# A two-layer gMLP and forgetting-attention trunk on one core: x loaded ahead of small broadcasts, the residual reloaded in mixer 2, one finished tile per unit of the last product, key projection ahead of the first softmax

## The chip, the cores and the metric

The kernel runs on one core of a Trainium2 chip. Its metric is the device time of one execution in microseconds (us). Before the change that is 2215.34 us, the median of three runs (2212.86 to 2218.98). The core's engines each work through a queue of their own: TensorE (PE) multiplies matrices, VectorE (DVE), ScalarE (ACT) and GpSimd (POOL) work on tiles in SBUF and PSUM, and SyncE (SP) issues most of the transfers (DMAs) between DRAM and SBUF.

## The reference

The input x is 1024 tokens of width 1024, all fp32. Two layers work on it, one after the other. What they compute, cut to its core:

```python
# layer A: gMLP mixer and memory attention, then a gated FFN with a causal convolution
z = rmsnorm(x, a_norm1) @ a_w_in                      # 768 u, 768 v, 256 memory queries
u, vv, q_mem = gelu(z[:768]), gelu(z[768:1536]), z[1536:]
tok = u * (tril(w_s) @ rmsnorm(vv, v_norm) + b_s)     # blocks of 128 tokens, 4 groups
x = x + concat(tok, memory_attention(q_mem, mem)) @ a_w_out
x = x + conv_ffn(rmsnorm(x, a_norm2), ...)            # 1024 -> 2 x 2816 -> 1024
# shared keys, values and forget gates, from the x of here
kvf = rmsnorm(x, kv_norm) @ w_kv                      # 768 k, 768 v, 12 gate logits
log_f_cum = cumsum(log_sigmoid(f_logit + b_f))
# layer B: causal attention with a decay bias, 12 heads of 64, and memory attention
z = rmsnorm(x, b_norm1) @ b_w_q                       # 768 q, 256 memory queries
logits = q @ k.T / 8 + log_f_cum[q] - log_f_cum[k]    # causal
x = x + concat(softmax(logits) @ v, memory_attention(...)) @ b_w_out
x = x + conv_ffn(rmsnorm(x, b_norm2), ...)
out = rmsnorm(x, final_norm)
```

## The kernel before

Every fp32 operand of a large product is split in two parts, a rounded high part and the rest (`split_to`, `split_new`, `wconv`, `opnd`: ACT casts the high part, DVE or POOL subtracts it for the low one), and each product is three matmuls: high by high, high by low, low by high. TensorE has 10,657 matmuls and transposes in all. SBUF tiles of 128 rows by 1024 fp32 (512 KB) come from one pool of 33 buffers, drawn with `xt_()` and named X in the profile; a new tile waits until the buffer that it gets is no longer read. Tiles of the tag `nb` have three buffers.

The Python code emits the instructions of all engines, and a scheduler arranges each engine's queue when the kernel is built, except for those marked with `tc.keep_in_program_order`: these keep the order in which the code emits them. The matmuls and transposes of the mixers are marked so while `strict[0]` is set, and loads made with `ld` while `dpin[0]` is set:

```python
        ins = nc.sync.dma_start(dst, src)
        if dpin[0]:
            tc.keep_in_program_order(ins)
```

**The start.** SP loads weights and x tiles (line 184, in `ld`). `x_in(i)` squares two token tiles on ACT, transposes them on PE and splits them into `xh`, `xl`; behind each pair, `vv_g` makes the first v projections of these tokens (lines 1077 to 1080). `dpin[0] = False` stands at line 1055, ahead of that loop. The broadcasts of a_b_s into `bsb` (line 1122, eight loads) and of b_f into `bf` (line 1226) are emitted later; the mixer and the gate logits read them.

**The FFN.** `ffn` is used by both layers. Its output product, `out_phase`, is cut in halves of its three dimensions and made of seven block products in place of eight: p1, p5, p6, p3, p7, p2 and p4, each over NU = 6 units of up to two 128-deep blocks. `prep` loads and splits the operands of a unit AHEAD = 2 units before it is multiplied; `both(x, y, pool)` splits x and y, one of them on POOL where `pool` is true (x in layer A, y in layer B, where `tm` is true), lines 799 and 800 are the cast and the subtraction. p2 ends the first four tiles of the result (`acc[0]` to `acc[3]`): `take` adds the bank of PSUM, and `on_done(j, acc[j])` hands the tile on. p4, the last product, ends the other four; its last TAILU = 2 units run tile by tile:

```python
            for j in range(4):
                on_done(j, acc[j])
            for u in range(NU - TAILU):
                run(a, "p4", u, False)
                before_last(u + 1)
```

In layer A `on_done` is `done_a`: the tile is split (`nh`, `nl`) and its square is added to a running sum (ACT squares, POOL adds, line 342). In layer B it is `finish`, the last norm and the store.

**The entry into attention.** Behind the first projections of layer B come the gate logits `fz`, log-sigmoid on ACT and DVE, VPRE = 8 steps of `mem_v` (three 256-wide matmuls each) on PE, the transposes of the gates, a scan on DVE, and a store and broadcasts of the sums by way of DRAM (`cdram`). Then LOOK first steps of scores (`s_tasks`) are emitted, and the next key and query projection, `proj_kq`, is drawn ahead until its own count of time reaches PRE = 5000 ns, in steps of 432 ns.

**The attention loop.** 48 steps (a head and a pair of query blocks each) merge scores, softmax and values; projections that are still to be made (`fills`) are laid between them, at a rate that spreads what is left of each over the steps up to its due step.

**The second mixer.** `tail` loads each head pair's attention result `o` from DRAM and splits it, and rebuilds the residual x from its halves, one tile per `merge_next`, with a POOL addition (line 1600):

```python
        eng.tensor_tensor(t, f32(xl[n]), f32(xh[n]), ALU.add)
```

The merged result is multiplied with `b_w_out` (`mix_part`, `mix_out`), and the second FFN follows. `xdram` is a DRAM buffer for x, to which the mixers store it and from which `load_xT` reads it for the FFN's sum.

Of the kernel before, what the change touches and what calls it, by code (L numbers as in the profile page):

```python
# [13 lines left out]
ALU = mybir.AluOpType  # L14
AX = mybir.AxisListType

P = 128
# [25 lines left out]
TRATE = 1.0  # L43
KQD = 5
EVY = 0
PRE = 5000.0
MQD = (41, 45)
MEMT = 45
CONVK = 12
VPRE = 8  # L50
NORD = (0, 4, 1, 5, 2, 6, 3, 7)
POOLED = (0, 3, 4, 5, 6)
HK = NFF // 2
# [6 lines left out]
def kernel(  # L60
# [33 lines left out]
    nc = tc.nc  # L94
# [22 lines left out]
    def xt_(dt=F32, shape=(P, S)):  # L117
        return xp.tile(list(shape), dt, tag="X", name=nm("X"))
# [12 lines left out]
    def f32(ap):  # L131
        return ap.bitcast(F32)
# [48 lines left out]
    dpin = [False]  # L181

    def ld(dst, src):
# [3 lines that stand above are left out]
# [330 lines left out]
    def drain(g):  # L517
        for _ in g:
            pass
# [154 lines left out]
    def ffn(ops, ssum, first, w_out, cvs, on_done, tp, tm, before_last=lambda stage: None):  # L674
# [128 lines left out]
        def both(x, y, pool=False):  # L803
            return opnd(x, pool and not tm), opnd(y, pool and tm)

        def tt(out, x, y, op=ALU.subtract):
            nc.vector.tensor_tensor(out, x, y, op)  # L807
            return out
# [3 lines left out]
        def prep(name, u):  # L812
# [30 lines left out]
            if name == "p2":  # L843
                return both(la(0, 1, u), lb(1, 0, u), True)
            a22, b21 = la(1, 1, u), lb(1, 0, u)
            return both(a22, tt(b21, b21, kept[u][1]), True)

        steps = [("p1", u) for u in range(NU)]
        for u in range(NU + 1):
# [55 lines left out]
        def out_phase(cg):  # L905
# [4 lines left out]
            def run(bank, p, u, start):  # L910
                i = steps.index((p, u))
                ahead(i + 1 + AHEAD)
                op = ready.pop((p, u))
                for j in range(4):
                    mms(bank, op, u, j, start)
# [35 lines left out]
                if u == 2:  # L951
                    before_last(0)
            take(c, 0, 0)
            for j in range(4):
                on_done(j, acc[j])
            for u in range(NU - TAILU):
                run(a, "p4", u, False)
                before_last(u + 1)
            ahead(len(steps))
            for j in range(4):  # L960
# [91 lines left out]
    ws_raw = tp.tile([P, 4, P], F32, tag="T2", name="ws_raw", bufs=3)  # L1052
    ld(ws_raw, a_w_s[0].rearrange("g t s -> t g s"))

    dpin[0] = False
    vg = {}
    sv = cp.tile([P, KT, 3], F32, name="sv")

# [18 lines left out]
    for i in range(4):  # L1077
        if i < 3:
            x_in(i + 1)
        drain(vv_g(0, (2 * i, 2 * i + 1)))  # L1080
    rm = mem_norm(tp, mtok, "P", pbufs[0])
    rb = cp.tile([P, S], F32, name="rb_a", tag="rb", bufs=1)

# [35 lines left out]
               [(2, 0, P)], [(2, 0, 64), (3, 64, P)], [(3, 0, P)]]  # L1119
    for f in range(6):  # L1120
        for g, lo_, hi_ in fgroups[f]:
            ld(bsb[lo_:hi_, f, :], a_b_s[0, g:g + 1, :].broadcast_to([hi_ - lo_, P]))

    memq.append(mem_q(1))

# [40 lines left out]
    for f in range(6):  # L1166
# [19 lines left out]
        u = xt_()  # L1186
# [36 lines left out]
        return a[:, :n], a[:, n:], b[:, :n], b[:, n:]  # L1223

    bf = cp.tile([P, 12], F32, name="bf")
    nc.sync.dma_start(bf, b_f.rearrange("(o h) -> o h", o=1).broadcast_to([P, 12]))
    nh, nl, ssums = [], [], []

    def done_a(n, xn):
        h, l = xt_(F32R), xt_(F32R)  # L1230
        split_to(h, l, xn)
        nh.append(h)
        nl.append(l)
        if n == 0:
            ssums.append(tp.tile([P, S], F32, tag="T", name=nm("S"), bufs=4))
        add_square(tp, ssums[0], xn, n, "T", 4)
# [357 lines left out]

    xT = {}

    def merge_next(eng):
        n = NORD[len(xT)]
        t = xt_()
        eng.tensor_tensor(t, f32(xl[n]), f32(xh[n]), ALU.add)  # L1600
        xT[n] = t

    mix = {}

    def tail():
        for i, p in enumerate(PSEQ):
            o = tp.tile([P, S], F32, tag="nb", name=nm("o"), bufs=3)
            nc.sync.dma_start(o, odram[p * P:(p + 1) * P, :])
            if i < 5:
                merge_next(nc.gpsimd)  # L1610
            mix[p] = split_new(o)
        while len(xT) < KT:
            merge_next(nc.gpsimd)
        mh, ml = ({p: mix[p][i] for p in PSEQ} for i in range(2))
        for n in NORD[:NPRE]:
            yield from mix_part(wst.use(("o", n), 1)[0], PSEQ, mh, ml, xT[n])
# [77 lines left out]
```

## Time and profile before

| | us | share of the span |
|---|---|---|
| median of three runs | 2215.34 | |
| the profiled execution | 2213.66 | |
| its span, first to last instruction | 2211.9 | 100% |
| PE busy (matmuls) | 2123.1 | 96% |
| PEld busy (weight loads, beside PE) | 1784.4 | 81% |
| DVE busy | 1727.9 | 78% |
| ACT busy | 1036.2 | 47% |
| POOL busy | 820.2 | 37% |

The mean granted clock of TensorE was 0.990 of full speed. The DMA engines moved 243.54 MB, nearly all by one queue whose packets took 34.5% of the time of 16 engines. All rows below come from one profiled execution; times are microseconds from the start of its span, and L12 is line 12 of the kernel. The mean granted clock of a stretch is given as PEclk, where 1.00 is 2.4 GHz and 0.50 is 1.2 GHz. An idle time is put down to the instruction whose result came last, shown behind an arrow.

### The profile page before, as it was taken

The page shows a single profiled execution, that of the slowest core. Times are in us where ns is not written, and L with a number is a line of the kernel's source. Part 1 is how long each engine was busy: PE and PEld are TensorE (multiplying, and loading weights), DVE is VectorE, ACT ScalarE, POOL GpSimd, SP SyncE. Part 2 cuts the span into 40 slices and gives each one's busy share as a digit, 9 for nine tenths or more (in the row PEclk, how much of TensorE's full clock was granted, in tenths as well). Part 3 has the DMA queues.
Part 4 walks back from the last instruction along what each step waited for, and adds up shares of the span by engine and source line. Part 5 has one row for each costly group of instructions (what it writes and reads, how often), then busy time and mean ns, then how long its engine had stood idle before and what let it go on. Part 6 is the DMA issues. An engine that isn't in the chain of part 4 may idle for free.

```text
span 2211.9 us, 29423 instructions
## 1 busy us (share of the span) xinstructions
PE 2123.1 (96%) x10657; PEld 1784.4 (81%) x10657; DVE 1727.9 (78%) x2544; ACT 1036.2 (47%) x1732; POOL 820.2 (37%) x602
## 2 busy tenths in 40 slices
PE   7999999999999999999899999789999999999998
PEld 6997877888888888878788788668788888888886
DVE  4745658999999898666776676786899999987966
ACT  6562344444444434343555564664544444444433
POOL 2321443444444100451545454555344444420033
PEclk9999999999999999999999999999999999999999
DMA  5311232222222775413322333323222222257463
GB/s 175 105 30 29 76 105 68 77 86 86 86 86 86 262 251 194 144 39 91 103 79 87 88 95 86 104 70 111 74 80 81 83 79 86 86 199 265 149 204 116
DMA packets 219165, 243.54 MB, mean 110 GB/s; under 512 B 10074, under 2 KB 155648, under 8 KB 219020
## 3 DMA queue, kind: packets, MB, share of 16 engines
q1 hardware_dynamic: 218880, 241.63, 34.5%
q8 instruction: 84, 1.38, 0.3%
q14 instruction: 61, 0.50, 0.1%
q10 hardware_dynamic: 140, 0.04, 0.0%
HBM read 192.29 MB, written 38.85 MB: 104 GB/s over the span
## 4 chain that ended last, share of the span: by engine, by line
PE 39%; DVE 6%; DMA 2%; ACT 2%; issue 2%; POOL 1%; SPq 0%; DVEq 0%; POOLq 0%; ACTq 0%
PE pa L137 35%; PE pc L137 2%; PE pc L143 2%; DMA nb<-cdram 1%; DVE P L1379 1%; DVE X L347 1%; ACT P L1385 1%; DVE X L430 1%; DVE PTl L347 1%; DMA wr<-in_b_w_q_dram 0%; DMA X<-xdram 0%; ACT PTh L346 0%; DVE X L423 0%; ACT Pm L481 0%; POOL P L459 0%
## 5 line engine op out<-in xcount | busy, mean ns | idle before, releaser
L137 PE MATMUL pa<-X,wo 128*128 128x512 f32 x3696 | 841.9, 389 | 3.7 <-ACT X L346 2.5
L137 PEld LDWEIGHTS pa<-X,wo 128*128 128x128 f32 x3696 | 692.8, 188 | 150.3 <-ACT X L346 4.3
L137 PE MATMUL pa<-X,X 128*128 128x512 f32 (+2 forms) x1868 | 440.9, 379 | 13.6 <-DVE sm L1379 8.6
L137 PEld LDWEIGHTS pa<-X,X 128*128 128x128 f32 x1868 | 340.7, 189 | 83.2 <-DVE sm L1379 8.5
L137 PE MATMUL pa<-X,wh 128*128 128x512 f32 (+1 forms) x1216 | 354.3, 400 | 9.9 <-DVE X L347 8.6
L641 POOL TENSOR_TENSOR wo<-raw,wo 128x512 fp32r<-128x512 f32 x132 | 210.9, 1598 | 204.2 <-ACT wo L639 177.2
L137 PEld LDWEIGHTS pa<-X,wh 128*128 128x128 f32 x1216 | 219.2, 190 | 55.1 <-DVE X L347 11.4
L641 POOL TENSOR_TENSOR wo<-ws,wo 128x512 fp32r<-128x512 f32 x88 | 153.1, 1740 | 288.9 <-ACT wo L639 288.9
L799 ACT CAST X<-ro 128x1024 fp32r<-128x1024 f32 (+1 forms) x142 | 131.0, 964 | 175.4 <-DVE ro L807 72.3
L137 PE MATMUL pa<-X,wl 128*128 128x512 f32 (+1 forms) x608 | 194.5, 399 | 0.1
L639 ACT CAST wo<-ws 128x512 fp32r<-128x512 f32 x176 | 108.3, 617 | 175.5 <-PE pa L137 164.2
L800 POOL TENSOR_TENSOR X<-ro,X 128x1024 fp32r<-128x1024 f32 (+1 forms) x24 | 60.3, 2517 | 344.8 <-ACT X L799 330.3
L800 DVE TENSOR_TENSOR X<-ro,X 128x1024 fp32r<-128x1024 f32 (+1 forms) x118 | 145.2, 1257 | 32.6 <-ACT X L799 29.7
L218 POOL TENSOR_TENSOR wl<-wr,wh 128x1024 fp32r<-128x1024 f32 (+1 forms) x41 | 103.5, 2524 | 175.8 <-ACT wh L217 171.2
L639 ACT CAST wo<-raw 128x512 fp32r<-128x512 f32 x132 | 81.8, 620 | 185.2 <-PE pa L137 176.2
L137 PE MATMUL pa<-wh,X 128*128 128x256 f32 (+1 forms) x800 | 166.8, 287 | 0.9 <-ACT X L1072 0.9
L137 PEld LDWEIGHTS pa<-wh,X 128*128 128x128 f32 x800 | 131.8, 189 | 2.8 <-ACT X L1072 1.2
L137 PEld LDWEIGHTS pa<-X,wl 128*128 128x128 f32 x608 | 110.2, 189 | 20.0 <-DVE wl L218 0.5
L347 DVE TENSOR_TENSOR PTl<-pc,PTh 128x512 fp32r<-128x512 f32 (+1 forms) x152 | 90.7, 601 | 37.5 <-ACT PTh L346 36.2
L137 PE MATMUL pa<-wl,X 128*128 128x256 f32 (+1 forms) x400 | 113.3, 283 | 2.3 <-POOL wl L218 2.3
L459 POOL TENSOR_SCALAR P<-P,sm 128x128 f32<-128x128 f32 (+3 forms) x96 | 77.3, 806 | 91.9 <-DVE sm L1386 81.4
L1385 ACT ACTIVATE P<-P,sm 128x128 f32<-128x128 f32 (+3 forms) x96 | 74.7, 778 | 74.8 <-DVE sm L1379 73.1
(196 smaller groups left out, 3345.9 us busy)
## 6 DMA issues: line engine op xcount, KB each, us to landing
ro<-hdram SPq DMA_DIRECT2D x67, 512.0 KB
raw<-in_a_ffn_in_dram SPq DMA_DIRECT2D x44, 512.0 KB
hdram<-X SPq DMA_DIRECT2D x44, 512.0 KB
raw<-in_b_ffn_in_dram SPq DMA_DIRECT2D x44, 512.0 KB
ro<-in_a_ffn_out_dram SPq DMA_DIRECT2D x35, 512.0 KB
ro<-in_b_ffn_out_dram SPq DMA_DIRECT2D x32, 512.0 KB
X<-X SPq DMA_DIRECT2D x80, 128.0 KB
xdram<-X SPq DMA_DIRECT2D x16, 512.0 KB
```

The costliest lines, as they stand in the source:

```text
L137: ins = nc.tensor.matmul(*a, **k)
L143: ins = nc.tensor.transpose(*a)
L218: eng.tensor_tensor(lo, raw, f32(hi), ALU.subtract)
L347: nc.vector.tensor_tensor(lo, src, f32(hi), ALU.subtract)
L430: nc.vector.tensor_tensor(dl[e][a, cs], qf[a], f32(dh[e][a, cs]), ALU.subtract)
L459: nc.gpsimd.tensor_scalar(p, p, rinv, 1.0, ALU.mult, ALU.mult)
L639: nc.scalar.copy(h, src)
L641: eng.tensor_tensor(l, src, f32(h), ALU.subtract)
L799: nc.scalar.copy(h, src)
L800: (nc.gpsimd if pool else nc.vector).tensor_tensor(l, src, f32(h), ALU.subtract)
L1379: nc.vector.tensor_tensor_reduce(p[:, c0:c1], ps[:, c0 - k0:c1 - k0], bias, 1.0, 3.0e38 if mn is None else mn, ALU.add, ALU.min, m2)
L1385: nc.scalar.activation(p[:, :n], p[:, :n], AF.Exp, bias=mn, scale=-1.0, accum_out=rs)
```

## The change

It has five parts. The first half of `out_phase`'s hand-over is emitted in the unit loop of p4, one tile behind each of its first four units, where it was emitted for four tiles at once ahead of that loop. The low part of a22 in p4 of layer A is made by DVE instead of POOL; layer B stays as it was. At the start, `ld` keeps the program's order until the first v projections are emitted, the eight broadcasts of `bsb` move from SP to ACT's queue and keep their place there, and the one of `bf` keeps its place on SP. In the entry into attention, 16 steps of `mem_v` instead of 8 are drawn ahead of the gate's transposes, and `proj_kq` is drawn to 10,000 ns instead of 5,000 ahead of the loop. `done_a` also stores each finished x tile to `xdram`, and `merge_next`, the POOL addition, becomes `load_next`, a load of that tile by SP.

```diff
@@ -43,11 +43,11 @@
 TRATE = 1.0
 KQD = 5
 EVY = 0
-PRE = 5000.0
+PRE = 10000.0
 MQD = (41, 45)
 MEMT = 45
 CONVK = 12
-VPRE = 8
+VPRE = 16
 NORD = (0, 4, 1, 5, 2, 6, 3, 7)
 POOLED = (0, 3, 4, 5, 6)
 HK = NFF // 2
@@ -843,7 +843,7 @@
             if name == "p2":
                 return both(la(0, 1, u), lb(1, 0, u), True)
             a22, b21 = la(1, 1, u), lb(1, 0, u)
-            return both(a22, tt(b21, b21, kept[u][1]), True)
+            return both(a22, tt(b21, b21, kept[u][1]), tm)
 
         steps = [("p1", u) for u in range(NU)]
         for u in range(NU + 1):
@@ -951,10 +951,9 @@
                 if u == 2:
                     before_last(0)
             take(c, 0, 0)
-            for j in range(4):
-                on_done(j, acc[j])
             for u in range(NU - TAILU):
                 run(a, "p4", u, False)
+                on_done(u, acc[u])
                 before_last(u + 1)
             ahead(len(steps))
             for j in range(4):
@@ -1052,7 +1051,6 @@
     ws_raw = tp.tile([P, 4, P], F32, tag="T2", name="ws_raw", bufs=3)
     ld(ws_raw, a_w_s[0].rearrange("g t s -> t g s"))
 
-    dpin[0] = False
     vg = {}
     sv = cp.tile([P, KT, 3], F32, name="sv")
 
@@ -1078,6 +1076,7 @@
         if i < 3:
             x_in(i + 1)
         drain(vv_g(0, (2 * i, 2 * i + 1)))
+    dpin[0] = False
     rm = mem_norm(tp, mtok, "P", pbufs[0])
     rb = cp.tile([P, S], F32, name="rb_a", tag="rb", bufs=1)
 
@@ -1119,7 +1118,8 @@
                [(2, 0, P)], [(2, 0, 64), (3, 64, P)], [(3, 0, P)]]
     for f in range(6):
         for g, lo_, hi_ in fgroups[f]:
-            ld(bsb[lo_:hi_, f, :], a_b_s[0, g:g + 1, :].broadcast_to([hi_ - lo_, P]))
+            tc.keep_in_program_order(nc.scalar.dma_start(
+                bsb[lo_:hi_, f, :], a_b_s[0, g:g + 1, :].broadcast_to([hi_ - lo_, P])))
 
     memq.append(mem_q(1))
 
@@ -1223,10 +1223,12 @@
         return a[:, :n], a[:, n:], b[:, :n], b[:, n:]
 
     bf = cp.tile([P, 12], F32, name="bf")
-    nc.sync.dma_start(bf, b_f.rearrange("(o h) -> o h", o=1).broadcast_to([P, 12]))
+    tc.keep_in_program_order(
+        nc.sync.dma_start(bf, b_f.rearrange("(o h) -> o h", o=1).broadcast_to([P, 12])))
     nh, nl, ssums = [], [], []
 
     def done_a(n, xn):
+        nc.sync.dma_start(xdram[n * P:(n + 1) * P, :], xn)
         h, l = xt_(F32R), xt_(F32R)
         split_to(h, l, xn)
         nh.append(h)
@@ -1594,11 +1596,10 @@
 
     xT = {}
 
-    def merge_next(eng):
+    def load_next():
         n = NORD[len(xT)]
-        t = xt_()
-        eng.tensor_tensor(t, f32(xl[n]), f32(xh[n]), ALU.add)
-        xT[n] = t
+        xT[n] = xt_()
+        nc.sync.dma_start(xT[n], xdram[n * P:(n + 1) * P, :])
 
     mix = {}
 
@@ -1607,10 +1608,10 @@
             o = tp.tile([P, S], F32, tag="nb", name=nm("o"), bufs=3)
             nc.sync.dma_start(o, odram[p * P:(p + 1) * P, :])
             if i < 5:
-                merge_next(nc.gpsimd)
+                load_next()
             mix[p] = split_new(o)
         while len(xT) < KT:
-            merge_next(nc.gpsimd)
+            load_next()
         mh, ml = ({p: mix[p][i] for p in PSEQ} for i in range(2))
         for n in NORD[:NPRE]:
             yield from mix_part(wst.use(("o", n), 1)[0], PSEQ, mh, ml, xT[n])
```

## Rows read from the trace of the kernel before

**Rows 1.** The chain of waits near the end: start us, us, what

```profile
1986.43 9.60 DMA X<-xdram
...
2024.69 2.72 PE pc L137 x12
```

**Rows 2.** Busy time by stage: window; length, engines (x instructions), PEclk, DMA share, GB/s

```profile
943.61:968.50 24.89, 21.38 (x95) 16.42 (x94) 16.09 (x14) 13.02 (x18) 17.20 (x8) 1.00 0.10 33
1033.28:1056.00 22.72, 13.92 (x69) 11.01 (x69) 14.50 (x30) 7.80 (x14) 7.16 (x7) 0.86 0.39 106
1056.00:1230.00 174.00, 162.98 (x1004) 141.07 (x1003) 128.61 (x393) 102.40 (x225) 91.78 (x96) 0.99 0.31 87
1441.00:1475.00 34.00, 23.68 (x121) 17.82 (x120) 32.64 (x37) 21.31 (x51) 26.20 (x25) 0.95 0.19 65
```

**Rows 3.** The timeline of SP's queue at the start: start us, us, what

```profile
1.71 6.13 SPq L184 DMA_DIRECT2D wr<-in_a_w_in_dram  x3
7.89 4.86 SPq L184 DMA_DIRECT2D bsb<-in_a_b_s_dram  x8
...
13.27 3.13 SPq L184 DMA_DIRECT2D X<-in_x_dram  x6
```

**Rows 4.** PE's timeline at the start (in brackets: us waited, and for what)

```profile
18.02 0.48 PE L143 MATMUL pa<-ident,X 128*128 128x128 f32 x1 [7.45 <-DMA X<-in_x_dram]
...
22.37 0.36 PE L137 MATMUL pa<-wh,X 128*128 128x256 f32 x1
```

**Rows 5.** POOL's timeline at the start

```profile
16.75 2.85 POOL L218 TENSOR_TENSOR wl<-wr,wh 128x1024 fp32r<-128x1024 f32 x1 [5.25 <-ACT wh L217]
```

**Rows 6.** Groups by line, 925 to 970 us: xcount | busy, mean ns | idle before

```profile
L137 PE MATMUL pa<-X,X 128*128 128x512 f32 x148 | 36.2, 395 | 3.5 <-POOL X L800 1.9 <-DVE X L800 1.6
...
L342 POOL TENSOR_TENSOR S<-S,sq 128x1024 f32<-128x1024 f32 x5 | 13.0, 2604 | 19.8 <-ACT sq L338 19.8
...
L800 POOL TENSOR_TENSOR X<-ro,X 128x1024 fp32r<-128x1024 f32 x3 | 8.2, 2726 | 0.0
...
L800 DVE TENSOR_TENSOR X<-ro,X 128x1024 fp32r<-128x1024 f32 x3 | 6.0, 2004 | 2.8 <-ACT X L799 2.8
```

**Rows 7.** DVE's timeline in the second mixer

```profile
1460.70 1.22 DVE L347 TENSOR_TENSOR X<-o,X 128x1024 fp32r<-128x1024 f32 x1
```

**Rows 8.** PE's timeline at the entry into attention

```profile
1030.26 3.03 PE L137 MATMUL pa<-W,X 128*128 128x256 f32 x24
...
1036.24 1.87 PE L143 MATMUL pc<-ident,fz 128*12 128x128 f32 x8 [2.96 <-DVE fz L1511]
...
1051.99 0.33 PE L143 MATMUL pc<-ident,P 128*128 128x128 f32 x1 [2.44 <-POOL P L459]
...
1055.20 0.69 PE L143 MATMUL pc<-ident,P 128*128 128x128 f32 x2 [2.88 <-POOL P L459]
```

**Rows 9.** A window of PE alone: length, PE busy, PEclk, DMA share, GB/s

```profile
1036.10:1039.50 3.40, 3.26 (x16) 0.50 0.00 0
```

**Rows 10.** PE's timeline at the end of the attention loop

```profile
1420.66 1.22 PE L137 MATMUL pa<-X,X 128*128 128x256 f32 x4 [5.38 <-DVE sm L1379]
```

**Rows 11.** POOL's timeline at the end of the attention loop

```profile
1414.67 2.81 POOL L1600 TENSOR_TENSOR X<-X,X 128x1024 f32<-128x1024 f32 x1
```

**Rows 12.** DVE's timeline in the same stretch

```profile
1414.33 5.94 DVE L430 TENSOR_TENSOR X<-qf,X 64x512 fp32r<-64x512 f32 x4
```

**Rows 13.** Groups by line, the whole span

```profile
L430 DVE TENSOR_TENSOR X<-qf,X 64x512 fp32r<-64x512 f32 x40 | 39.2, 993 | 1.1 <-ACT X L429 0.3
```

**Rows 14.** Groups by line, 1441 to 1475 us

```profile
L1600 POOL TENSOR_TENSOR X<-X,X 128x1024 f32<-128x1024 f32 x7 | 17.6, 2523 | 0.0
...
L347 DVE TENSOR_TENSOR X<-o,X 128x1024 fp32r<-128x1024 f32 x6 | 16.4, 2734 | 0.3 <-ACT X L346 0.2
...
L137 PE MATMUL pa<-X,wh 128*128 128x512 f32 x32 | 11.8, 450 | 8.9 <-DVE X L347 8.6 <-ACT X L346 0.3
```

**Rows 15.** The timeline of SP's queue in the second mixer

```profile
1445.12 13.92 SPq L1608 DMA_DIRECT2D o<-odram  x4
```

## The prediction

> **What bounds the kernel now.** Read in this order: the stage table, then the waits and timelines of the stages in which TensorE isn't full, then the chain of waits. TensorE (PE) is busy for 2123.1 of the span's 2211.9 us, so time can come only from the stages where it waits. In steady product work one 128x512 matmul takes 2.72 / 12 = 0.227 us [rows 1], and no part of the change alters how many of them there are. The stage table [rows 2] shows four places with holes: the last product of the first FFN (943 to 968 us), the entry into forgetting attention (1033 to 1056: 13.92 of 22.72 busy), the attention loop (1056 to 1230: 162.98 of 174) and the second mixer (1441 to 1475: 23.68 of 34, while VectorE is busy for 32.64). A fifth is the start, where PE waits for x. The two FFN bodies are full and the change leaves their products alone.
>
> **The start.** SP issues three weight loads, then eight broadcasts of a_b_s in 4.86 us, then one of b_f, and only at 13.27 the six remaining x tiles [rows 3]. PE stands 7.45 us for the third x tile and starts its transposes at 18.02 [rows 4]. With the loads pinned until the first v projections are through, the third weight load comes behind x as well, so x can be issued from about 7.5 to 7.9 us: 13.27 - 7.89 = 5.4 us earlier, which is the upper end. What is late next: the first v matmul (22.37) [rows 4] needs the split weights, and POOL's half of them ends at 16.75 + 2.85 = 19.60 [rows 5]; the second pair of x tiles now asks ACT and DVE for its squares and splits in the same microseconds, which pushes these weights back. If they slip by 1.9 us, only 22.37 - 21.5 = 0.9 us is left: the lower end. I take 3.5, nearest to the case in which the second weight half (needed some 1.4 us into the matmuls) sets the start near 18.9. The eight broadcasts now cost ACT's queue some 4.86 us around 100 us, beside PE work, with their result wanted only in the mixer much later: 0, at worst 1.
>
> **The last product of the first FFN.** Four finished tiles used to be handed on at once ahead of it; now one goes after each of its first four units. Each hand-over is an ACT copy and square, a DVE subtraction and a POOL addition. In this stage PE waited 3.5 us, 1.9 for POOL's subtraction and 1.6 for DVE's [rows 6]. The change also takes the subtraction for a22 (six units) from POOL, where one takes 2.73 us, to DVE, where the undisturbed form takes 1.22 [rows 7]. Upper end 3.5. Lower end -2: DVE gets six more of 1.22 us (7.3 us), of a stage in which it was idle for 24.89 - 16.09 = 8.8 us [rows 2], so it fits, but just. I take 2.5, nearer the waits that name POOL and the queue behind it. The eight stores of x (512 KB each, on SP) meet a DMA share of 0.10 [rows 2]: 0. Queued behind them on SP are only weight loads of the next stage; a store that waits for a late tile holds these by no more than the tile's own lateness.
>
> The row first: the DVE subtractions of this stage took 2.00 us in the mean, against 1.22, beside POOL additions of 2.60 [rows 6]. The Trainium skill ("SBUF — State Buffer", section "Who interferes with whom") says that a VectorE instruction with two SBUF inputs and a GpSimd instruction that reads SBUF hold one port pair exclusively, the later one blocked for the whole of the other. By that rule the moved subtractions meet the square additions that stay on POOL, and this term could be 0; that is case B below.
>
> **The entry into attention.** Eight more groups of three 256-wide matmuls (mem_v, second half) go ahead of the gate's transposes. The first half took 3.03 us for its 24 [rows 8], and PE then waited 2.96 us for the log-sigmoid chain: the hole is filled almost exactly. The k projection goes from 12 to 24 units (432 ns is the code's own count, 5184 to 10368), so 24 more matmuls x 0.227 = 5.45 us run ahead of the first softmax's transposes. From the gate's transposes to those transposes it is 1051.99 - 1036.24 = 15.75 us, set by scan, two DMAs and softmax, not by PE. In it PE will have at most 1.87 (the gate's transposes, at half clock in this row) + 1.0 (eight half-width logit matmuls) + 10.9 (48 of k) = 13.8 us, so the softmax's transposes are not delayed, and 2.96 + 2.44 + 2.88 us of waits [rows 8] shrink to some 5. The 5.45 us are work that the loop behind need not do; it is paced over its steps. PE there is busy 94% [rows 2], but part of that loop waits on DVE's softmax, so less work isn't all less time. Upper end 5.45 + 1.7, the second term being what the half clock of 1036 to 1039.5 cost [rows 9], if the filled hole keeps the clock up. Lower end -1, if the loop is bound by latency and the earlier weight conversions sit in DVE's queue ahead of the softmax. I take 3.5, about two thirds of 5.45.
>
> **The second mixer.** Eight POOL additions that rebuild x from its halves go; eight 512 KB loads on SP come. Two gains. At 1414.67 the first addition (2.81 us) stands ahead of a softmax normalisation on POOL and beside four q subtractions on DVE, which take 5.94 us [rows 10 to 12]; in the mean such a one takes 0.99 [rows 13], so 4.0, and PE's wait of 5.38 us there shrinks by about 2. With the normalisation earlier as well I take 2.5 (1 to 4.5). From 1441 on, seven additions lie beside six subtractions of o that take 2.73 us in the mean, 16.4 together; the one without an addition beside it took 1.22 [rows 7, 14]. DVE loses 16.4 - 6 x 1.22 = 9.1 us of its 32.64. PE waited 8.9 us, 8.6 of it for exactly these [rows 14]. What is late next is the load of o: two buffers, one load per 4.53 us now ((13.92 - 0.33) / 3) [rows 15], and PE's own 23.68 us. Upper end 34 - 23.68 = 10.3; lower end 3; I take 7, nearer the 8.9. The reloads themselves need a free X buffer. Sixteen are freed at once when the last projection is done (1411), as nothing keeps xh and xl for the additions, so most of the loads can run between 1411 and 1441, ahead of the o loads. Cost 0 if so; otherwise case D.
>
> **The last FFN's end.** The same spreading there moves `finish` for four tiles between units. PE shows no hole, and the subtraction's engine doesn't change in that layer. 0 (-2 to 0.5): the last tiles could find DVE busy with the fourth of these.
>
> **The sum.** 3.5 + 2.5 + 3.5 + 2.5 + 7 = 19.0 us. The profiled execution's own time is 2213.66 (span 2211.9 and 1.8 around it), 1.7 below the median of 2215.34. 2213.66 - 19.0 = 2194.7, so 2195. All upper ends: 5.4 + 3.5 + 7.1 + 4.5 + 10.3 + 0.5 = 31.3, 2182; all lower ends: 0.9 - 1 - 2 - 1 + 1 + 3 - 2 = -1.1, 2215.
>
> **The rivals.**
> B, the DVE and POOL pair keeps the first FFN's last stage as slow as it is (its row above): 2213.66 - 16.5 = 2197.
> C, the waits pass to the next link: the start is held by the weights (2 instead of 3.5), the loop by latency (0), the wait at 1420 goes to 1 and the o loads leave 4: 2 + 2.5 + 0 + 1 + 4 = 9.5, so 2204. For it: DVE is on most waits of the loop. Against it: in the mixer DVE's own queue is the wait, and it is relieved directly.
> D, the reloads collide with the o loads on SP's one queue. A 512 KB load from the same buffer landed after 9.60 us when the queue was full [rows 1]. With two buffers that is a load per (9.60 + 1.22) / 2 = 5.4 us against 4.53: 0.9 x 4 = 3.6 us lost where 7 were to be won: 2213.66 - 12 + 3.6 = 2205. Against it: the slots come free 30 us ahead. It includes the case that the change doesn't do what it says, x being rebuilt or reloaded with the same wait.
> E, slower: the clock in the attention loop. With 5.45 us of fill gone ahead, each step of the first 19 has less to lay over the softmax; a longer idle stretch ahead of a step lets the clock fall to 1.2 GHz, as it did at 1036 after 2.96 us of idling, for 3.4 us at a loss of 1.7 [rows 8, 9]. It decides from 19.0 / 1.7, about 11 further falls, on; one in each of 19 steps would be 32 us, so 2213.66 - 19 + 32 = 2227. Against it: 5.45 us are 3% of the stage's PE work.
> F, all goes well and the clock stays up too: 2185.
>
> **Chances.** Likeliest case 0.46 (its own range 2189 to 2201), B 0.10, C 0.24, D 0.10, E 0.06, F 0.04. A measurement of this kernel can tell about 0.3%, 6.6 us. Faster: 0.46 + 0.10 + 0.20 of C + 0.05 of D + 0.04 = 0.85; same: 0.04 of C + 0.05 of D = 0.09; slower: 0.06. The range of 8 in 10 leaves out E, F and the slow edge of C and D: 2186 to 2209.
>
> **What would show it.** Start: the six x loads issued by 8 to 11 us and the first v matmul by 19 to 20; wrong if it stays past 21. First FFN: PE's waits for X at line 800 near the last product under 1 us, and no POOL rows there for that line. Entry: no PE wait ahead of the gate's transposes, the first softmax's transposes still some 15.8 us behind them; wrong if they come over 1 us later. Loop: the stretch up to the last projection shorter by 2 to 5 us; E if the granted clock falls more than a few times more. Mixer: the o subtractions at 1.2 to 1.4 us and the stretch of 34 us down to 25 to 29; D if PE's waits there name the loads of o instead of DVE. The forecast as a whole is wrong if the mixer's stretch doesn't shrink, as it holds half of the sum.

## The result and the profile after

The changed kernel takes 2189.14 us (median of four executions, 2184.55 to 2190.27), the kernel before 2214.66 us beside it (2212.86 to 2218.98): a ratio of 0.9878, 95% interval 0.9866 to 0.9891, or about 26 us. The forecast was 2195, with a range of 2186 to 2209. The profiled execution took 2189.55 us with a span of 2187.5, which is 24.4 us less than the span of before.

Both kernels execute the same matmuls, so one can find the same matmul in both profiles and subtract the two starting times. That lead, in us, tells where the time came from:

| matmul | start before | lead of the changed kernel |
|---|---|---|
| transposes behind layer A's first v projections | 54.8 | 5.1 |
| layer A's other v projections | 105.0 | 3.7 |
| layer A's u projections | 180.3 | 2.1 |
| ahead of the first FFN's last product | 934.9 | 1.4 |
| its end | 962.0 | 6.0 |
| gate's transposes | 1036.2 | 5.5 |
| first softmax's transposes | 1052.0 | 1.9 |
| fifth transpose of probabilities | 1061.5 | 6.6 |
| attention loop | 1178.8 | 14.0 |
| attention loop | 1398.6 | 15.8 |
| its end | 1428.1 | 18.1 |
| second mixer's product | 1475.7 | 24.7 |
| last FFN, sum | 2003.6 | 24.2 |

The stage table of the changed kernel, with windows that hold the work of those of before (the loop's are cut at other places, since its order differs): window, length, busy time of each engine, PEclk, DMA share, GB/s.

```profile
942.19:962.50 20.31, 20.31 (x97) 16.75 (x96) 16.45 (x15) 12.07 (x15) 9.00 (x4) 1.00 0.22 79
1027.76:1050.00 22.24, 18.13 (x89) 14.49 (x88) 15.05 (x36) 8.48 (x16) 8.24 (x9) 0.92 0.42 108
1050.00:1216.00 166.00, 155.73 (x984) 135.63 (x982) 127.00 (x387) 101.54 (x223) 92.70 (x95) 1.00 0.34 91
1422.97:1450.32 27.35, 23.58 (x121) 17.33 (x120) 22.47 (x37) 21.03 (x51) 7.22 (x16) 1.00 0.61 214
```

Against [rows 2]: PE is now busy for the whole of the first FFN's last product, the entry is fuller (18.13 of 22.24), and the second mixer takes 27.35 us for the work that took 34.00, with VectorE down from 32.64 to 22.47 and the DMAs up from 0.19 to 0.61.

The start, from SP's and then PE's timeline (start, us, what), against [rows 3, 4]: only two weight loads stand ahead of x, which is issued from 6.55 on instead of 13.27, and the first v matmul comes at 15.81 instead of 22.37.

```profile
1.71 0.99 SPq L184 DMA_DIRECT2D wr<-in_a_w_in_dram  x2
6.55 4.21 SPq L184 DMA_DIRECT2D X<-in_x_dram  x6
...
15.81 0.56 PE L137 MATMUL pa<-wh,X 128*128 128x256 f32 x1
```

The groups of the first FFN's last product, 923 to 968 us, against [rows 6]. PE waits for nothing; the subtraction of line 800 is on VectorE alone, and takes 1.22 us there. What is slow now is the hand-over's own subtraction (line 347: 2.18 us, beside POOL's squares), and nobody waits for it:

```profile
L137 PE MATMUL pa<-X,X 128*128 128x512 f32 x150 | 35.4, 392 | 0.0
L347 DVE TENSOR_TENSOR X<-X,X 128x1024 fp32r<-128x1024 f32 x8 | 17.3, 2177 | 2.4 <-ACT X L346 2.4
...
L800 DVE TENSOR_TENSOR X<-ro,X 128x1024 fp32r<-128x1024 f32 x5 | 6.0, 1218 | 1.6 <-ACT X L799 1.6
```

PE's timeline at the entry into attention, against [rows 8]. The gate's transposes no longer wait, but a new wait of 4.03 us for the key projection's weights follows them, and the first softmax's transposes come 1050.06 - 1030.72 = 19.3 us behind them, not 15.75:

```profile
1030.72 1.04 PE L143 MATMUL pc<-ident,fz 128*12 128x128 f32 x8
1031.51 1.54 PE L137 MATMUL pa<-X,X 128*128 128x256 f32 x8
1037.08 1.26 PE L137 MATMUL pa<-X,wh 128*128 128x512 f32 x4 [4.03 <-ACT wh L217]
...
1050.06 0.49 PE L143 MATMUL pc<-ident,P 128*128 128x128 f32 x3
```

The end of the loop (PE's and VectorE's timeline, against [rows 10, 12]) and the groups of the second mixer, 1423 to 1451 us (against [rows 14]). The wait of 5.38 us is 3.34, and the four q subtractions on VectorE take 3.92 us instead of 5.94, which is the same 2 us. The subtractions of o take 1.23 us instead of 2.73; PE's waits are 3.8 instead of 8.9 us, and the larger part now names ACT's casts of o, which in turn wait for the loads of o:

```profile
1402.87 0.89 PE L137 MATMUL pa<-X,X 128*128 128x256 f32 x4 [3.34 <-DVE sm L1381]
...
1398.57 3.92 DVE L430 TENSOR_TENSOR X<-qf,X 64x512 fp32r<-64x512 f32 x4
...
L137 PE MATMUL pa<-X,wh 128*128 128x512 f32 x33 | 11.9, 439 | 3.8 <-ACT X L346 2.3 <-DVE X L347 1.1
L347 DVE TENSOR_TENSOR X<-o,X 128x1024 fp32r<-128x1024 f32 x6 | 7.4, 1226 | 3.9 <-ACT X L346 3.8
L346 ACT CAST X<-o 128x1024 fp32r<-128x1024 f32 x6 | 6.3, 1047 | 3.3 <-DMA o<-odram 3.3
```

SP's queue there (against [rows 15]), and the cast that waited for the load issued at 1428.20: reloads of x stand between the loads of o. One of the eight was issued at 1382.69, the other seven only from 1422.13 on: ahead of them the queue stood 8.6 us at a store of an attention result (1421.59) that waited for VectorE.

```profile
1422.13 0.54 SPq L1602 DMA_DIRECT2D X<-xdram  x1
...
1428.20 0.32 SPq L1609 DMA_DIRECT2D o<-odram  x1
1428.57 0.42 SPq L1602 DMA_DIRECT2D X<-xdram  x1
...
1434.24 1.04 ACT L346 CAST X<-o 128x1024 fp32r<-128x1024 f32 x1 [1.19 <-DMA o<-odram]
```

### The profile page after: what moved, and what is told of

Same layout as the page of the kernel before. It is cut to its first block, busy times and chain, and to the rows that moved or that the text cites. A ratio compares the mean times of both kernels' runs of the same rounds, so it can differ in the third digit from the quotient of the medians.

```text
span 2187.5 us, 29468 instructions
## 1 busy us (share of the span) xinstructions
PE 2121.6 (97%) x10657; PEld 1784.9 (82%) x10657; DVE 1714.2 (78%) x2550; ACT 1035.7 (47%) x1732; POOL 785.1 (36%) x588
## 4 chain that ended last, share of the span: by engine, by line
PE 80%; DVE 8%; DMA 5%; ACT 4%; issue 2%; POOL 1%; SPq 0%; ACTq 0%; DVEq 0%; POOLq 0%
PE pa L137 72%; PE pc L137 5%; PE pc L143 2%; DMA nb<-cdram 1%; DVE P L1381 1%; DMA X<-xdram 1%; DVE X L347 1%; DMA ro<-hdram 1%; DVE X L430 1%; ACT P L1387 1%; DVE PTl L347 1%; DMA o<-odram 0%; ACT PTh L346 0%; ACT Pm L481 0%; DVE X L800 0%
## 5 line engine op out<-in xcount | busy, mean ns | idle before, releaser
L800 POOL TENSOR_TENSOR X<-ro,X 128x1024 fp32r<-128x1024 f32 (+1 forms) x18 | 45.5, 2535 | 339.4 <-ACT X L799 336.6
```

The source lines that it names most:

```text
L800: (nc.gpsimd if pool else nc.vector).tensor_tensor(l, src, f32(h), ALU.subtract)
```

## The experiments

All of them start from the changed kernel; "back" undoes one part. Executions of one kernel differ by 3 to 14 us, and most of that goes with the clock: over 78 executions of 13 kernels, an execution whose mean granted clock is 0.001 lower takes 1.65 us longer than others of its kernel (the slope of a straight line through the differences from each kernel's own means). The last column uses this slope: the time at equal clock, against the mean of the eight executions of the changed kernel. A difference in it is good to about 2.4 us (95%). What an edit itself does to the clock is taken out of this column too.

| kernel | median us | ratio to before, 95% | mean clock | at equal clock |
|---|---|---|---|---|
| before (24 executions beside these) | 2216.0 | | 0.9893 | +22.1 |
| changed, and again | 2189.1, 2189.4 | 0.9878 [0.9866, 0.9891], 0.9885 [0.9864, 0.9907] | 0.9921 | 0 |
| mix_back | 2202.2 | 0.9943 [0.9924, 0.9963] | 0.9886 | +7.9 |
| mix_junk | 2197.4 | 0.9918 [0.9894, 0.9942] | 0.9908 | +5.6 |
| pre_back | 2195.1 | 0.9910 [0.9886, 0.9935] | 0.9918 | +4.3 |
| vpre_back | 2190.6 | 0.9882 [0.9867, 0.9897] | 0.9925 | +2.6 |
| conv_early | 2186.9 | 0.9886 [0.9865, 0.9906] | 0.9924 | +0.9 |
| p4_pool | 2191.9 | 0.9886 [0.9871, 0.9901] | 0.9912 | +1.4 |
| p4_block | 2190.9 | 0.9879 [0.9864, 0.9894] | 0.9912 | -0.1 |
| start_back | 2192.4 | 0.9894 [0.9877, 0.9912] | 0.9925 | +4.5 |
| start_bsb | 2194.1 | 0.9904 [0.9887, 0.9922] | 0.9910 | +4.1 |
| x_late | 2187.6 | 0.9873 [0.9859, 0.9886] | 0.9922 | -0.8 |
| best | 2190.5 | 0.9884 [0.9869, 0.9900] | 0.9905 | -1.2 |

**The changed kernel once more (again).**

> The changed kernel once more, unaltered, as the yardstick for the others. Its stages should come out as in its first profile, to within what the clock does. In that profile TensorE was at 1.2 GHz in five stretches ahead of the end (171 to 174.5, 976.6 to 986.9, 1038 to 1041.5, 1348.7 to 1352.1, 1403.3 to 1406.7), 23.9 us together, and in the profile of before in seven, 34.0 us; one such stretch of 3.4 us at full work costs 1.7 us. If the falls belong to the program, the same five stand here and the 5 us of difference to before belong to the change. If they come and go between executions of one program, one or two of them are missing or new here, and of the 24.4 us that the span lost some 2 to 5 are luck of the two profiles compared.

The span was 2187.6 us, as in the first profile. The stretches at 1.2 GHz were not the same: 171.8 to 175.2, 977.3 to 987.6, 1035.4 to 1042.2, 1349.4 to 1352.8, 1376.7 to 1380.1 and 1404.0 to 1410.8, together 34.1 us against 23.9. So the falls vary from execution to execution, and two profiles must not be compared fall by fall. That this execution came out no slower is due to the second mixer, where 2.5 us were made up: the loads of o, issued in the same order with the same reloads between them, landed earlier, and ACT waited 0.8 instead of 3.3 us for them. The load that corresponds to the slow one shown above was cast 4.5 us after its issue, without a wait (SP's and ACT's timeline):

```profile
1430.55 0.32 SPq L1609 DMA_DIRECT2D o<-odram  x1
...
1435.01 1.03 ACT L346 CAST X<-o 128x1024 fp32r<-128x1024 f32 x1
```

**The mixer: the addition back on GpSimd (mix_back), and additions that nothing reads (mix_junk).**

```diff
 # mix_back
-        xT[n] = xt_()
-        nc.sync.dma_start(xT[n], xdram[n * P:(n + 1) * P, :])
+        t = xt_()
+        nc.gpsimd.tensor_tensor(t, f32(xl[n]), f32(xh[n]), ALU.add)
+        xT[n] = t
 # and done_a without the store to xdram
 # mix_junk: reloads as in the changed kernel, and in tail()
             mix[p] = split_new(o)
+            junk = tp.tile([P, S], F32, tag="P", ...)
+            nc.gpsimd.tensor_tensor(junk, f32(mix[p][0]), rb, ALU.add)
```

> The residual is rebuilt from its halves by GpSimd again (no store to xdram in the first FFN, no reload); all else as in the changed kernel. My theory: the 9 us that the stretch from the last projection's end to 1475 (of before) lost are GpSimd's additions standing beside VectorE's subtractions. The subtraction of o takes 2.7 us again instead of 1.2, the stretch 1441 to 1475 is back at 34 us from about 27, PE's wait ahead of the softmax normalisation near 1403 is back at 5.4 us from 3.6, and the time is 2198 (ratio to before 0.992). Rival: most of that gain came from what the earlier parts moved (the order of the loop's end, the clock): then the time stays within 3 us of the changed kernel's.

> The changed kernel with its reloads, and six GpSimd additions of 128x1024 that nothing reads, each released by the rounded high part of o, at the moment at which VectorE's subtraction of that o is released too. If a GpSimd addition beside it is what makes the subtraction slow, the six take 2.4 to 2.7 us instead of 1.2, and 5 to 8 us of the mixer's gain go: 2195 to 2198. If the subtractions were slow in the kernel before for another reason (the buffers of the residual, the DMAs, ACT), they stay at 1.2 to 1.5 us and the time at 2189 to 2191.

Undoing the part cost 13 us in the median, 7.9 at equal clock; from 1315 to 1475 the profile lost 9.0 us to the changed kernel's. The wait ahead of the normalisation is back at 5.38, and the four q subtractions beside POOL's first addition at 5.95. Adding the useless additions cost 8 us in the median and 5.6 at equal clock; their profile, the fastest of the four executions, lost 3.3 us in the stretch. The rows say how. First mix_back, PE's, VectorE's and POOL's timeline and the group (1425 to 1458 us):

```profile
1404.23 1.01 PE L137 MATMUL pa<-X,X 128*128 128x256 f32 x3 [5.38 <-DVE sm L1380]
...
1425.36 3.33 DVE L347 TENSOR_TENSOR X<-o,X 128x1024 fp32r<-128x1024 f32 x1 [0.20 <-ACT X L346]
...
1425.25 2.36 POOL L1601 TENSOR_TENSOR X<-X,X 128x1024 f32<-128x1024 f32 x1
...
L347 DVE TENSOR_TENSOR X<-o,X 128x1024 fp32r<-128x1024 f32 x6 | 15.1, 2520 | 0.6 <-ACT X L346 0.5
```

and the same of mix_junk (1423 to 1454 us):

```profile
1423.56 1.23 DVE L347 TENSOR_TENSOR X<-o,X 128x1024 fp32r<-128x1024 f32 x1 [0.20 <-ACT X L346]
...
1430.04 2.35 DVE L347 TENSOR_TENSOR X<-o,X 128x1024 fp32r<-128x1024 f32 x1
...
1423.61 3.43 POOL L1614 TENSOR_TENSOR jk<-X,rb_b 128x1024 f32<-128x1024 f32 x1
...
1428.90 2.41 POOL L1614 TENSOR_TENSOR jk<-X,rb_b 128x1024 f32<-128x1024 f32 x1
...
L347 DVE TENSOR_TENSOR X<-o,X 128x1024 fp32r<-128x1024 f32 x6 | 11.5, 1916 | 1.0 <-ACT X L346 0.9
```

The later of the two stands until the earlier is done. In mix_back POOL starts at 1425.25 and ends at 1427.61; VectorE, released at 1425.36, ends at 1428.69, 1.08 us behind POOL. In mix_junk VectorE was first at 1423.56 and took its 1.23 us; POOL's addition beside it took 3.43 instead of 2.4. At 1428.90 POOL was first, and VectorE's subtraction took 2.35. The six subtractions took 1.9 us in the mean, less than the 2.4 to 2.7 that I expected, because in mix_junk only three of them stood behind an addition of POOL (2.32 to 2.89 us); the other three took 1.23 to 1.35. The rival, that the residual's buffers or the DMAs slowed the subtraction, is refuted: in mix_junk the reloads and the residual's buffers are as in the changed kernel. The Trainium skill ("SBUF — State Buffer", section "Who interferes with whom") says that a VectorE instruction with two SBUF inputs and a GpSimd instruction that reads SBUF contend for a port pair held exclusively, and that the order of issue decides which one is blocked; these rows agree, in both orders.

**The entry: the key projection (pre_back), the memory's values (vpre_back), the weights ahead of the scan (conv_early).**

```diff
-PRE = 10000.0        # pre_back
+PRE = 5000.0
-VPRE = 16            # vpre_back
+VPRE = 8
+    wst.conv(wst.at["mv"] + 3)      # conv_early, ahead of the scan
     cum = tp.tile([P, S], F32, tag="nb", name="cum", bufs=3)[:H]
```

> PRE back at 5000: 12 instead of 24 steps of the key projection ahead of the first softmax; mem_v stays at 16. The changed kernel gained 14.3 - 5.5 = 8.5 us between the gate's transposes and 1230, where I had taken 3.5 for the whole entry. If the filled wait for the log-sigmoid chain (mem_v) did most of it, this kernel loses 0 to 3 us to the changed one. If the key projection did (its 5.45 us leave the loop whole, and the waits of 2.9 us with the half clock behind them, 1053 to 1060, come back without it), it loses 5 to 8 us: 2194 to 2197.

> VPRE back at 8 (half of mem_v ahead of the gate's transposes), PRE stays at 10000. With PRE at 5000 the stretch from the gate's transposes on lost 7 us, so of the 8.5 us that the changed kernel gained there about 1.5 are left for mem_v. The wait of 2.96 us for the log-sigmoid chain is back, but the second half of mem_v now lies where PE waited 4.03 us for the weights of the key projection (near 1037). My expectation: the two cancel, the time is within 2 us of the changed kernel's 2189 and PE's wait for the weights is down to 0.5 us. The rival, the prediction's own wording (mem_v fills a hole that nothing else fills): 3 to 5 us slower, 2192 to 2194.

> The weights of the first key projection are converted ahead of the scan instead of behind it; all else as changed. In the changed kernel PE waited 4.03 us near 1037 for exactly these (VectorE: scan to 1034.8, scaling to 1035.9; ACT's cast to 1037.0), and the clock fell behind that wait for 3.4 us (1.7 us of work). The first softmax's probabilities were ready at 1045.7, its transposes came at 1050.1 behind the 48 matmuls of the projection. If that wait is on the path, the transposes come 2.5 to 4 us earlier (the subtraction of 1.2 us now stands ahead of the scan) and the time is 2184 to 2187. If the softmax's own chain (scan, two DMAs, VectorE) sets the entry, the matmuls run earlier, PE waits later, and the time stays at 2188 to 2190.

With PRE back, PE's timeline has the two waits of the first softmax again, and the kernel lost 7.4 us to the changed one's profile between 1010 and 1164 (4.3 in the whole at equal clock, 5.9 in the medians):

```profile
1042.14 0.33 PE L143 MATMUL pc<-ident,P 128*128 128x128 f32 x1 [1.06 <-POOL P L459]
1045.38 0.69 PE L143 MATMUL pc<-ident,P 128*128 128x128 f32 x2 [2.91 <-POOL P L459]
```

With VPRE back the wait for the log-sigmoid chain returns and the wait for the weights goes; by 1056 that profile is 0.35 us behind the changed one's, 0.29 of which it had at 995 already. In time it is 2.6 us behind at equal clock, which is at the edge of what these runs can tell, and 1.2 in the median:

```profile
1031.00 1.11 PE L143 MATMUL pc<-ident,fz 128*12 128x128 f32 x8 [2.95 <-DVE fz L1513]
1037.91 1.21 PE L137 MATMUL pa<-X,wh 128*128 128x512 f32 x4 [0.20 <-ACT wh L217]
```

In conv_early the wait of 4.03 us is gone and the first softmax's transposes come at 1041.59, 13.3 us behind the gate's. But what was hidden behind the wait now shows:

```profile
1028.29 1.04 PE L143 MATMUL pc<-ident,fz 128*12 128x128 f32 x8 [1.09 <-DVE fz L1513]
...
1041.59 0.27 PE L143 MATMUL pc<-ident,P 128*128 128x128 f32 x1
1044.31 0.44 PE L143 MATMUL pc<-ident,P 128*128 128x128 f32 x2 [2.45 <-POOL P L459]
1051.11 0.55 PE L143 MATMUL pc<-ident,P 128*128 128x128 f32 x3 [2.24 <-POOL P L459]
1053.69 1.22 PE L137 MATMUL pa<-X,X 128*128 128x512 f32 x2 [1.57 <-DVE sm L1381]
```

2.45 + 2.24 + 1.57 us of waits for the softmax's chain (POOL's normalisation, VectorE's maxima) follow, the lead of 8.5 us at the first softmax's transposes is 1.6 at 1067, and that is less than the 2.4 that the profile had at the gate's. So the 2 to 5 us did not come: the softmax's chain sets the entry, and the rival that I had named for it holds. The time alone doesn't decide it: the median, 2186.9, lies where the first theory had it, the mean of the five executions (2184.1 to 2197.9), 2189.5, where the rival had it.

**The first FFN's last product: the engine (p4_pool) and the spreading (p4_block).**

```diff
-            return both(a22, tt(b21, b21, kept[u][1]), tm)        # p4_pool
+            return both(a22, tt(b21, b21, kept[u][1]), True)
+            for j in range(4):                                    # p4_block
+                on_done(j, acc[j])
             for u in range(NU - TAILU):
                 run(a, "p4", u, False)
-                on_done(u, acc[u])
```

> The low half of a22 in the last product of the first FFN on GpSimd again; the hand-over of the tiles stays one per unit. The changed kernel lost all four waits of this product (1.48, 0.69, 1.30, 0.91: 4.4 us). If the engine of this subtraction is the cause, GpSimd (its six of 2.5 us, four additions of squares, one weight) gives back 2 to 4.4 us: 2191 to 2193, and a wait for line 800 on POOL is in the profile. If the spreading is the cause, the waits stay away: 2189.

> Four tiles handed on at once ahead of the last product again, in both layers; the subtraction of a22 stays on VectorE. If the spreading is the cause of the 4.4 us, VectorE stands through four subtractions slowed by GpSimd's squares before it comes to the operands of the second and third unit, and 1.5 to 4 us come back (2191 to 2193). If the engine is, 0 to 1 us. The last FFN, where I took the spreading at 0 (-2 to 0.5): the changed kernel's span lost 0.5 us around 1972 to before, ahead of p1, so no change is expected there.

PE's timeline of each kernel, its one wait in this product, p4_pool first:

```profile
957.63 6.87 PE L137 MATMUL pa<-X,X 128*128 128x512 f32 x29 [1.98 <-DVE X L800]
```

```profile
945.04 5.51 PE L137 MATMUL pa<-X,X 128*128 128x512 f32 x23 [0.44 <-DVE X L800]
```

The kernel before had four such waits, 4.4 us counted from start to start of the matmuls. Either half of the edit alone takes a good part of them away: the engine all but 0.7 us, the spreading all but 2.1, about half. With POOL's subtraction back, PE waits for VectorE: it stood behind POOL (2.27 us in the mean for its line 800). In the whole neither half can be told from zero.

**The start: all of it back (start_back), and the broadcasts on ACT alone (start_bsb).**

```diff
 # both: the loads' order is free again
+    dpin[0] = False
     vg = {}
...
         drain(vv_g(0, (2 * i, 2 * i + 1)))
-    dpin[0] = False
 # start_back also: bsb by ld on SP, bf not kept in order
```

> The start as before: the loads' order free after the weights, the broadcasts of a_b_s and b_f on SP ahead of six x tiles. The first v matmul comes 5 us later (22.4 instead of 17). But the changed kernel had given back 1.0 us at 89.7 (a wait for weights that GpSimd splits, 1.92 instead of 0.91) and 1.6 at 171 (a fall of the clock behind a wait that both kernels have) by 180. So with the start undone I expect 2 to 4 us at 200 and in the whole (2191 to 2193); if the head start survives untouched (the rival, and nearly the upper end of my term), 5 us: 2194.

> The loads' order is free again at the start, the broadcasts of a_b_s stay on ACT's queue. Only one weight load then stands ahead of the six x tiles on SP. If moving the broadcasts alone did it, the first v matmul comes at 17 to 18.5 (15.8 in the changed kernel, 22.4 before) and the time is within 2 us of 2189. If keeping the program's order did it, x comes as late as before, and the time is 2192 to 2194.

Undoing the start cost 3.3 us in the median, 4.5 at equal clock: 5.4 us at 29, of which 3.4 were left at 802 in the profile. Moving the broadcasts alone was a miss for both theories: the first v matmul came at 17.17, as expected of that edit alone, and the time was still that of the start undone. SP's, POOL's, VectorE's, ACT's and PE's timeline of start_bsb:

```profile
1.71 5.67 SPq L184 DMA_DIRECT2D wr<-in_a_w_in_dram  x3
7.61 3.75 SPq L184 DMA_DIRECT2D X<-in_x_dram  x6
...
17.17 0.56 PE L137 MATMUL pa<-wh,X 128*128 128x256 f32 x1
...
16.75 2.87 POOL L218 TENSOR_TENSOR wl<-wr,wh 128x1024 fp32r<-128x1024 f32 x1 [5.26 <-ACT wh L217]
...
17.64 3.06 DVE L213 TENSOR_TENSOR wr<-wr,norms 128x1024 f32<-128x1024 f32 x1
...
20.73 1.05 ACT L217 CAST wh<-wr 128x1024 fp32r<-128x1024 f32 x1 [3.79 <-DVE wr L213]
21.69 1.05 ACT L1010 ACTIVATE jk<-X 128x1024 f32<-128x1024 f32 x1
...
28.17 1.50 PE L143 MATMUL pa<-ident,X 128*128 128x128 f32 x12 [1.55 <-DVE X L347]
```

The third weight load is again ahead of x, and so the scheduler put its conversion ahead of the second pair of x tiles on VectorE and ACT. VectorE's scaling stood beside POOL's subtraction (3.06 us), ACT waited 3.79 us for it with the squares of x queued behind, and by 29 the lead was gone (4.9 us behind the changed kernel). So the broadcasts off SP make x early (7.61 instead of 13.27), but the lead lasts only with the kept order, which puts the third weight behind x. Whether the kept order alone would do, with the broadcasts still on SP, no run here shows.

**Reloads behind the loads of o (x_late), and with the weights ahead of the scan (best).**

```diff
             nc.sync.dma_start(o, odram[p * P:(p + 1) * P, :])
-            if i < 5:
-                load_next()
             mix[p] = split_new(o)
```

> The eight reloads of x are emitted behind the six loads of o instead of between them; all else as changed. In the changed kernel ACT waited 3.3 us in the mixer for loads of o, and those that had a reload beside them landed after 4.4 to 6.1 us against 3.3 in the kernel before. If the reloads slow the loads of o (my case D, in part), these land in about 3.5 us, PE's wait for ACT's casts of o (2.3 us) goes, and the time is 2186 to 2188. If x then comes too late for the first finished tile of the mixer's product (wanted 26 us behind the first reload now), VectorE waits at the addition of x, and the time is 2190 or more.

> Both of these edits together: weights converted ahead of the scan, reloads behind the loads of o. If their gains add, 2182 to 2186; if neither was on the path, 2188 to 2190.

The edit does what it should: all eight reloads are issued from 1435.67 on, and ACT waits for no load of o any more (group of 1423 to 1450 us):

```profile
1435.67 4.40 SPq L1602 DMA_DIRECT2D X<-xdram  x8
...
L346 ACT CAST X<-o 128x1024 fp32r<-128x1024 f32 x6 | 6.3, 1049 | 0.0
```

The load issued at 1426.12 was cast from 1429.45 on, so it took at most 3.3 us; the one of the changed kernel shown above took 1434.2 - 1428.2 = 6.0. The stretch was 3.1 us shorter than in the changed kernel's profile, but 2.5 us of that came without any edit in the second profile of the changed kernel, with the reloads where they were. So the reloads between the loads of o don't by themselves explain the slow landings of the first profile; what does stays open. In the time neither x_late nor best can be told from the changed kernel, and no version here beats it.

## Why the prediction came out, step by step

**The sum.** 19.0 us were forecast. At equal clock the two kernels differ by 22.1; the undone parts add up to about the same (7.9 + 4.3 + 2.6 + 4.5 + 1.4 = 20.7), a sum that is good to some 8 us only, as all five are taken against the same mean. The rest of the 26.7 us between the means is the clock: 0.9921 against 0.9893, 2.8 x 1.65 = 4.6 us. This I had only as a part of case F. Fewer waits in front of PE left fewer chances for a fall; that the change did this is argued from the two means, not tested by itself. Case E (the loop's clock falls more often) did not come: between 1060 and 1400 there were two stretches at 1.2 GHz before, and one and two in the two profiles of the changed kernel. In the two profiles compared, the start kept 1.4 us at 934.9 where 3.5 were forecast, and the first FFN gave 4.6 where 2.5 were: that these two errors cancel is luck. What the profiles show beyond 19.0 comes from the entry and the loop.

**The start: the term held (4.5 at equal clock against 3.5), the next link was misread.** x was issued at 6.55 and the first v matmul came at 15.81, where I had said 19 to 20. Of the split weights, which I took as next in line, POOL's half was ready at 19.37, hardly earlier than before (19.60), and held nothing up; PE waited 0.81 us for VectorE's half, ready at 17.14. That isn't owed to the third weight's place: in start_bsb, where it stands ahead of x, both halves come within 0.3 us of these times. The first v matmul was 6.6 us early, but until 20.9 these matmuls followed each other at 0.21 us and at 0.12 from then on, as they did in the kernel before almost from the first. So 3.7 us were left at 24.5, and 5.1 at 54.8, as the kernel before waited 0.93 us at 30.98 where the changed one didn't. 1.0 went at 89.72, where PE waited 1.92 instead of 0.91 us (from start to start) for weights that POOL splits, 1.6 at 171 by a fall of the clock, which only some executions have, and 0.7 near 798 in this profile alone.

**The first FFN: right, undersized in the profiles.** 2.5 forecast, 4.6 in the leads; in the time neither of its halves could be told from zero. Case B was wrong in place: the holds of VectorE and POOL are there, but they fell on the hand-over's subtractions, which have slack, not on the operands.

**The entry and the loop: the term that was mis-sized most.** 3.5 forecast; the leads give 15.6 - 5.5 = 10.1 up to 1237 (of which one fall of the clock at 1230, 1.7 us, was in the profile of before alone), and the two undone edits 4.3 + 2.6 at equal clock. Two steps behind the number failed. I had the hole ahead of the gate's transposes filled by mem_v: it was, but the second half of mem_v had been covering the conversion of the key weights, and a wait of 4.03 us stood there instead. And I had the first softmax's transposes undelayed at 15.75 us behind the gate's: they came after 19.3, as 48 matmuls of the projection, begun late, stood ahead of them. That did no harm, as vpre_back and conv_early show: PE did useful work in place of the waits for the softmax. What paid was the key projection, whose 5.45 us the loop no longer had to do, and the waits of 2.44 and 2.88 us that it covered, the second with half clock behind it.

**The second mixer: right.** 7 forecast for the stretch, 34.00 - 27.35 = 6.65 in the profile; 2.5 for the wait ahead of it, 2.4 in the leads (5.38 to 3.34 us of wait, all of it in the q subtractions). mix_back shows the cause for both, mix_junk for the stretch. One step failed: I had the buffers freed at 1411 and most reloads ahead of the loads of o. Seven of eight were issued only from 1422.13 on, between the loads of o; what held them was not a buffer of X (they themselves waited for nothing longer than 0.4 us) but SP's queue, which stood 8.6 us at a store and then at the loads of o. The sign that I had named for case D, PE's waits there naming the loads of o, came in part: ACT's casts waited 3.3 us for loads that took up to 6.1 us. Whether the reloads did that is not shown. In the second profile, with the same order, ACT waited 0.8 us, and with the reloads behind (x_late) not at all; in the time the two kernels can't be told apart. Case D didn't turn the sign, since PE itself needs 23.6 us there.

**The last FFN: 0 forecast, 0.5 lost**, at PE's wait for the load of x into its sum (0.72 instead of 0.26 us near 1972, from start to start). That lies ahead of the spreading; from 2004 to the end the lead stays at 24.2, so the spreading itself was worth nothing, as forecast.

## What to carry to other kernels

When an engine's elementwise instruction takes twice its usual time in one stage, look at what the other engine of the pair (here VectorE and GpSimd) does in those microseconds, and take that work off the engines (here: a reload by DMA of a value that stands in DRAM) before tuning either. Fill a hole in front of the busy engine with work that has to be done anyway, but ask what the moved work was covering where it stood, since its old place becomes a hole: here the key projection paid, and the second half of mem_v hardly. Where a scheduler arranges the queues, an earlier load can lose its gain if the scheduler also moves another conversion ahead of more urgent work, as in start_bsb: look at both, and keep the order where it matters.

## What the runs showed of the hardware

The same wait is followed by a fall of the clock in the profile of one kernel and by none in that of the other. PE's timeline of before and the window behind it (PE busy, PEclk, DMA share, GB/s), an idle time of 2.37 us:

```profile
1230.37 0.63 PE L143 MATMUL pc<-ident,P 128*128 128x128 f32 x3 [2.37 <-DVE PTl L347]
...
1230.80:1234.10 3.30, 3.30 (x14) 0.51 0.68 130
```

and the same matmuls in the changed kernel, behind the same 2.37 us:

```profile
1216.38 0.52 PE L143 MATMUL pc<-ident,P 128*128 128x128 f32 x3 [2.37 <-DVE PTl L347]
...
1216.80:1220.10 3.30, 3.30 (x22) 1.00 0.69 129
```

14 matmuls instead of 22 in 3.30 us, at a granted clock of 0.51 (1.2 GHz) instead of 1.00 (2.4 GHz). The Trainium skill ("TensorE: Matmul & The Clock Gate", section "Part 1: The HAM clock gate") says that the gate doesn't keep step with a kernel, so that where a transition falls varies from run to run; the two windows agree, and so do the five and six falls in the two profiles of the changed kernel. For reading such runs it means that executions of one kernel spread by 3 to 14 us here (2207.8 at a mean clock of 0.992 to 2219.2 at 0.986 for the kernel before), and that effects of 2 us are better read from the same matmul in two profiles than from a median of four.
